# A two-layer decoder trunk on one core: masks written beside the rows and two tiles ahead, turnings of small tiles joined, key moves merged, the weight bound's passes regrouped

## Chip, core and metric

The kernel runs on one core of one Trainium2 chip. Its engines are named as in the profile: PE (TensorE matmul) and PEld (its weight load), DVE (VectorE), ACT (ScalarE), POOL (GpSimd) and SP (SyncE, which here only issues DMAs). The metric is the device time of one execution in microseconds (us), as the median over runs. A span is the time from the first to the last recorded instruction of a profiled execution.

## The reference

```python
D_MODEL, SEQ, DEPTH, N_MEM = 1024, 1024, 2, 256      # BATCH 1
FOX_HEADS, FOX_HEAD_DIM, MEM_HEADS, MEM_HEAD_DIM = 16, 64, 4, 128
...
def causal_multiscale_pool(u, pool_w, pool_scale): ...   # layer 0: trailing means of windows 2, 4, 8, 16
def shared_kv(x, w_kv_shared, b_forget): ...             # keys, values, cumulated log of the forget gates
def forgetting_attention(u, k, v, cum):
    # per head and block of 128 queries
    logits = q @ k.T * scale + (cum[t] - cum[s])
    logits = where(s <= t, logits, -inf)
    return softmax(logits) @ v
def memory_attention(q_mem, mem, w_mem_kv): ...          # 4 heads, softmax over 256 memory tokens
```

Each layer computes x = LayerNorm(alpha * x + W_out [main * silu(g_main); mem * silu(g_mem)]). In layer 0 main is the pooling branch, in layer 1 it is the forgetting attention (FoX) with 16 heads. Both layers have the memory attention.

## The kernel before

All products are made from operands split into a high part and a low part (and, in layer 0, a high part in another type), so that each product is a sum of two or three matmuls. A weight piece of 128x512 numbers is loaded into a buffer `raw` (four of them) or `B`, multiplied by a power of two in layer 1, and split. The power of two comes from a bound on the weights' absolute sums. This bound is worked out at run time: `look_ahead` (L231) loads a weight piece into one of eight slots in `lines[0]` by a DMA on POOL's queue (L240), seven pieces ahead, and has ACT sum the absolute values of the oldest (L244). There are 84 such pieces, 16 for the memory heads' weights and 68 for the others. `look_ahead` is called every 12 products in layer 0's output projection (L567) and at every eighth matmul of a slab (L327). After the last piece `send_bound(1)` (L267) sends the largest sum through DRAM to all partitions, and `scales_of_weights(1)` (L275) makes the scales from it in a chain of 12 small DVE instructions.

A slab (`slab`, L327) is 48 matmuls: one feature block of 128 columns of a weight matrix against all 1024 tokens. Keys (`k_units`), queries (`q_units`), values (`v_units`) and gates (`gate_units`) are slabs. Each is a generator that yields after each matmul, so slabs can be pumped in between other work.

Layer 0 has the pooling groups, the memory attention and the output projection `OutProj` (L512), whose `rest` ends with `norm` (L614). Layer 1 begins with the memory attention (`mem_attention`, L435): four query slabs in which the accumulators are evacuated by L431, L432 and L433, then for each of eight token tiles `probs` (L465 matmuls), a transposition, `values`, and four gate slabs as filling. Its outputs are multiplied by the gates on DVE (L509) and written to `y1d`. `scales_of_weights(1)` stands after it (L755). Then `start_units` runs: the first half of a key slab, `v_first` (the values of the first two pairs of heads and the forget logits, with weights in tiles MK; L804 is its matmul), the forget gates (L813 on), and the rest of the first pairs' keys and queries.

FoX (`fox`, L1043 on) runs over 16 heads, two to a pair, and over eight query tiles of 128 tokens in each, the largest (tile 7, 1024 keys) first. A step is one tile:

- `forget_rows` (L923) loads the next head's row of cumulated gates, in all partitions, into R (512 KB, L925, two buffers); this is called at the third tile of the head.
- `probs` (L928): POOL masks the diagonal block of R in place (L940), PE makes the logits in banks "L" (L295), one or two parts of up to 512 keys; DVE adds R and takes the least (L948) into a tile MK; ACT takes the exponential (L956) into a PSUM tile "T". The mask is held behind the mask of the tile before by `issue_after`.
- `halves`: ACT (L977) and DVE (L978) split the probabilities into a tile P, with the inverse of the sum (L966 or L968, then L969).
- `turn`: SP issues a DMA transposition of P into a tile T (L991). Tiles 2 and 0 are put behind tiles 3 and 1 in the same T.
- `values` (L1000): the products with V for four tiles at once; c=1 is tiles 4 to 7 (52 matmuls), c=0 is tiles 0 to 3. They come `LAG` = 5 steps behind, so that c=1 runs early in the next head's steps.
- `pair_out` (L1027): POOL multiplies the pair's outputs with the gates, SP writes them to `y1d` (L1029).

Between these, slabs of the coming pair are pumped in on PE. Their weights are split on POOL: L175 multiplies, L186 and L177 make the high and low halves. When a key slab is done, its halves have to lie in a second arrangement as well, high halves and low halves in other partitions: `move` (L858) does that with DMAs of 64 partitions on SP's queue. The keys' and queries' tiles are 16 lines of `lines[0]`, given out in turn by `qk`.

PE's order is written out by hand. The other engines' orders come from a scheduler, which also decides where DMAs stand in SP's and POOL's queues, except where an instruction is kept in program order or issued after another.

Of the kernel before, what the change touches and what calls it, by code (L numbers as in the profile page):

```python
# [12 lines left out]
F16 = mybir.dt.float16  # L13
# [65 lines left out]
def trunk_kernel(ctx, tc, x, xT, memT, win, wk, wv0, wv, wmk, wmv, wout, poolw, pscale, lng, lnb, bforget, out):  # L79
# [150 lines left out]

    def look_ahead():  # L231

        if lines:
            while len(landed) < 7:
                k, src = next(seen_of, (None, None))
                if k is None:
                    break
                r = lines[0][:, k % 8, :].bitcast(F32)
                r = r.rearrange("p (a b) -> p a b", a=4) if len(src.shape) == 3 else r[:, : src.shape[1]]
                nc.gpsimd.dma_start(r, src)  # L240
                landed.append((k, r))
            if landed:
                k, r = landed.pop(0)
                tc.keep_in_program_order(nc.scalar.activation(r, r, AF.Abs, accum_out=sums[:, k : k + 1]))  # L244
                if k == len(memory) + len(others) - 1:
                    send_bound(1)
# [50 lines left out]
    def slab(pieces_dram, X, evac, banks=("pj", 2)):  # L297
# [20 lines left out]
        for n, pc, part in order:  # L318
# [4 lines left out]
            for i in part:  # L323
                a, b = three(ws[pc], X)[i]
                for k in range(4):
                    seen[n] += 1
                    nc.tensor.matmul(  # L327
                        accs[n], a[:, k, :], b[:, pc * 4 + k, n * NH : (n + 1) * NH],
                        start=seen[n] == 1, stop=seen[n] == 3 * KT,
                    )  # L330
                    if sum(seen.values()) % 8 == 5:
                        look_ahead()
                    if seen[n] == 3 * KT:
                        evac(slice(n * NH, (n + 1) * NH), accs[n])
                    yield NH
# [99 lines left out]
    def mem_attention(l, X, kv, qtile, ytile, yd):  # L435
# [60 lines left out]
        with tc.manual_schedule(engines={PE}):  # L496
            for t in range(ST + 2):
                todo = [MVALUES if k in (5, 9) else 0 for k in range(t, ST + 2)]
                part = max(0, (fill.left + sum(todo)) / len(todo) - todo[0])
                if t < ST:  # L500
                    probs(t)
                fill.pump(part * 0.4)
                for h in range(MH):
# [8 lines left out]
    class OutProj:  # L512
# [39 lines left out]
        def products(self, accs, c, ys, apart=False):  # L552
# [9 lines left out]
            for a, nh, part in order:  # L562
                for i in part:
                    for k in range(4):
# [5 lines left out]
                        self.done += 1  # L570
                        if not self.l and self.done % 12 == 0:
                            look_ahead()
                        yield NH
# [160 lines left out]
    with tc.tile_pool(name="in1", bufs=1) as in1:  # L734
# [11 lines left out]

        line_at = [0]

        def qk():
            line_at[0] += 1  # L750
            return lines[0][:, line_at[0] % 16, :]

        kv = mem_kv(1)
        mem_attention(1, X, kv, xy, lambda: vt([P, S], F32), y1d[2])
        scales_of_weights(1)  # L755
        group[0] = 1
# [107 lines left out]
        def k_units(p):  # L864

            a, b, c, d = (qk() for _ in range(4))

            def evac(cols, acc):
                halves_out(a, b, cols, acc, QKSCALE)
                if cols.stop == S:  # L870
                    move(
                        (d, high64, a, high64), (c, low64, b, low64), (c, high64, a, low64), (d, low64, b, high64),
                        (a, high64, b, low64), (b, low64, d, high64),
                    )

            yield from slab(wk[p], X, evac)
            pairs[p] = [[(a, c), (b, d)]]

        def q_units(p):

            a, b, c = (qk() for _ in range(3))

# [37 lines left out]

        masked = []

# [5 lines left out]
        def probs(hd, i, R, sums, inverse, behind):  # L928
# [5 lines left out]
            q, kx, ky = pairs[hd // 2][hd % 2]  # L934
            L = (i + 1) * P
            qs = slice(i * P, L)
            p = MK([P, S], F32)
            with tc.issue_after(masked[-1]) if masked else nullcontext():
                masked.append(
                    nc.gpsimd.affine_select(R[:, qs], R[:, qs], [[-1, P]], ALU.is_ge, -NEG, base=0, channel_multiplier=1).ins  # L940
                )
            m = tiny(2)
            top = -NEG
            parts = [(0, L)] if L <= NH else [(0, 384), (384, L)] if L == 640 else [(0, NH), (NH, L)]
            for n, (lo, up) in enumerate(parts):
                lg = ps([P, NH], "L", 3)[:, : up - lo]
                mm3(lg, ((q[:, qs], kx[:, lo:up]), (q[:, qs], ky[:, lo:up])))
                nc.vector.tensor_tensor_reduce(p[:, lo:up], lg, R[:, lo:up], unq, top, ALU.add, ALU.min, m[:, n : n + 1])  # L948
                top = m[:, n : n + 1]
# [12 lines left out]
        def inverse_of(hd, i, n, sums):  # L962
# [7 lines left out]
            return r  # L970

        def halves(hd, i, es, r):

            L = (i + 1) * P
            pair = sb([P, 2 * S], "P", 4, F16)
            for lo, up, e in es:
# [6 lines left out]
        def turn(hd, i, two):  # L983

            n = 2 * i + 2
            if i in (2, 0):
                to = pt[hd, i + 1][:, n + 2 :, :]
            else:
                to = T([P, 2 * ST, P], F16)
            pt[hd, i] = to  # L990
            nc.sync.dma_start_transpose(to[:, :n, :], two[:, : n * P])  # L991
# [51 lines left out]
        def fox(following, out_proj):  # L1043
# [6 lines left out]

            ahead_R = forget_rows(0)
            for hd in range(HEADS + 1):
                pr, b = divmod(hd, 2)
# [15 lines left out]
                for i in range(ST if hd < HEADS else LAG):  # L1069
# [17 lines left out]
                    if i == 2 and hd < HEADS - 1:  # L1087
                        ahead_R = forget_rows(hd + 1)
                    if pr == 7:
                        step = b * ST + i  # L1090
# [100 lines left out]
```

## Time and profile before

| | us |
|---|---|
| median of 3 runs | 1229.65 |
| lowest and highest run | 1229.44, 1231.36 |
| the profiled execution's own time | 1231.59 |
| its span | 1229.9 |
| mean granted clock of PE, share of full speed | 0.988 |
| PE busy | 1181.9 |
| DVE busy | 777.1 |
| ACT busy | 700.8 |
| POOL busy | 266.6 |

The table is read as follows. The time of the profiled execution is 1.7 us over its span, since the work around the first and last instruction is not in the trace. Busy times of different engines overlap. An engine's busy time says how much it did and not whether another waited for it; for that one reads a wait and what released it. The order of the views in the next part follows this: whole span, stretches, waits, timeline.

In the profile "L" and a number is a line of the kernel before. "P<-T,s,P 128x512" names the output tile, the inputs and the shape of the output. "x4" counts instructions that follow each other. Brackets hold the engine's idle time ahead of the first of them, and what ended it.

### The profile page before, as it was taken

The page shows a single profiled execution, that of the slowest core. Times are in us where ns is not written, and L with a number is a line of the kernel's source. Part 1 is how long each engine was busy: PE and PEld are TensorE (multiplying, and loading weights), DVE is VectorE, ACT ScalarE, POOL GpSimd, SP SyncE. Part 2 cuts the span into 40 slices and gives each one's busy share as a digit, 9 for nine tenths or more (in the row PEclk, how much of TensorE's full clock was granted, in tenths as well). Part 3 has the DMA queues.
Part 4 walks back from the last instruction along what each step waited for, and adds up shares of the span by engine and source line. Part 5 has one row for each costly group of instructions (what it writes and reads, how often), then busy time and mean ns, then how long its engine had stood idle before and what let it go on. Part 6 is the DMA issues. An engine that isn't in the chain of part 4 may idle for free. (4 is left out here: it accounts for less than half of the span.)

```text
span 1229.9 us, 20105 instructions
## 1 busy us (share of the span) xinstructions
PE 1181.9 (96%) x7018; PEld 683.3 (56%) x7018; DVE 777.1 (63%) x1811; ACT 700.8 (57%) x1556; POOL 266.6 (22%) x437
## 2 busy tenths in 40 slices
PE   8999999999999998999799998998999999999997
PEld 4566676555555666556474455544455555455553
DVE  7534776375645467367743877667777878773754
ACT  6555774374574455787331776556666767685220
POOL 4000000000122110210243444443333422640000
PEclk9999999999999999999899999999999999999999
DMA  6233553243695655574825878976975887796340
GB/s 226 85 114 96 119 134 137 86 120 95 208 347 181 195 195 162 187 226 102 262 90 147 168 151 212 181 176 153 214 176 119 176 169 165 213 227 196 136 151 37
DMA packets 276773, 200.90 MB, mean 163 GB/s; under 512 B 213920, under 2 KB 227360, under 8 KB 276672
## 3 DMA queue, kind: packets, MB, share of 16 engines
q1 hardware_dynamic: 270080, 178.45, 54.7%
q0 software_dynamic: 6592, 21.17, 5.1%
q8 instruction: 55, 0.90, 0.3%
q14 instruction: 46, 0.38, 0.1%
HBM read 116.14 MB, written 22.61 MB: 113 GB/s over the span
## 5 line engine op out<-in xcount | busy, mean ns | idle before, releaser
L327 PE MATMUL pj<-A,w 128*128 128x512 f16 (+2 forms) x2928 | 673.3, 384 | 10.7 <-ACT w L171 5.3
L327 PEld LDWEIGHTS <-w 128*128 128x128 f16 (+1 forms) x2592 | 249.5, 98 | 290.1 <-issue 11.8
L956 ACT ACTIVATE T<-MK,s 128x512 f32<-128x512 f32 x192 | 111.4, 580 | 75.6 <-DVE s L948 59.3
L977 ACT ACTIVATE P<-T,s 128x512 f16<-128x512 f32 x192 | 102.3, 576 | 63.6 <-issue 33.1
L978 DVE SCALAR_TENSOR_TENSOR P<-T,s,P 128x512 f16<-128x512 f32 x192 | 111.7, 613 | 33.9 <-ACT P L977 32.8
L567 PEld LDWEIGHTS <-T 128*128 128x128 bf16 x736 | 71.0, 98 | 86.9 <-issue 6.0
L240 POOL DMA_DIRECT2D A<-in_win_dram x48 | 26.4, 551 | 372.2 <-PE pj L327 304.5
L192 DVE TENSOR_TENSOR w<-raw,w 128x512 bf16<-128x512 f32 x84 | 60.4, 720 | 61.6 <-PE pj L327 35.7
L295 PE MATMUL L<-A 128*128 128x512 f16 (+3 forms) x384 | 85.3, 326 | 8.3 <-DVE s L948 6.3
L948 DVE CUSTOM_DVE_ANT_0 MK<-L,R,scales 128x512 f32<-128x512 f32 (+3 forms) x128 | 80.3, 628 | 18.2 <-DMA R<-cumd 8.4
L327 PEld LDWEIGHTS pj<-A,w 128*128 128x128 f32 x368 | 69.3, 190 | 20.2 <-ACT A L191 3.6
L940 POOL TENSOR_SCALAR_AFFINE_SELECT R<-R 128x128 f32<-128x128 f32 x128 | 37.1, 296 | 170.9 <-DVE s L948 117.1
L1000 PE MATMUL O<-T,V 128*64 128x128 f16 (+1 forms) x1152 | 60.5, 227 | 10.0 <-DMA T<-P 9.8
L1000 PEld LDWEIGHTS <-V 128*64 128x64 f16 (+1 forms) x1152 | 53.5, 108 | 26.7 <-issue 12.4
L295 PEld LDWEIGHTS <-A 128*128 128x128 f16 x384 | 37.1, 98 | 52.3 <-issue 10.4
L191 ACT CAST w<-raw 128x512 fp32r<-128x512 f32 x84 | 52.0, 619 | 21.0 <-PE pj L327 12.0
L192 DVE TENSOR_TENSOR T<-T,T 128x1024 bf16<-128x1024 f32 x23 | 28.0, 1218 | 56.4 <-ACT T L191 41.8
L177 POOL TENSOR_TENSOR w<-B,w 128x512 f16<-128x512 f32 x54 | 62.4, 1156 | 3.5
L193 ACT CAST w<-raw 128x512 bf16<-128x512 f32 x84 | 52.0, 619 | 13.0 <-PE pj L327 12.4
L175 POOL TENSOR_SCALAR B<-B,scales 128x512 f32<-128x512 f32 x54 | 41.1, 774 | 83.6 <-DVE scales L285 29.8
L191 ACT CAST T<-T 128x1024 fp32r<-128x1024 f32 x23 | 24.1, 1046 | 57.4 <-DMA T<-y1d 36.2
L567 PE MATMUL pj<-B,T 128*128 128x512 bf16 (+1 forms) x192 | 54.3, 393 | 0.0
(263 smaller groups left out, 1796.0 us busy)
## 6 DMA issues: line engine op xcount, KB each, us to landing
raw<-in_win_dram SPq DMA_DIRECT2D x66, 256.0 KB, 2.8
A<-in_win_dram POOLq DMA_DIRECT2D x48, 256.0 KB, 5.2
raw<-in_wout_dram SPq DMA_DIRECT2D x40, 256.0 KB, 2.7
A<-A SPq DMA_DIRECT2D x72, 128.0 KB, 2.7
R<-cumd SPq DMA_DIRECT2D x16, 512.0 KB, 4.6
B<-in_win_dram SPq DMA_DIRECT2D x15, 512.0 KB, 4.8
y0d<-Y SPq DMA_DIRECT2D x12, 512.0 KB, 2.9
T<-y0d SPq DMA_DIRECT2D x12, 512.0 KB, 4.8
```

The lines of the kernel that those rows point to most:

```text
L177: nc.gpsimd.tensor_tensor(to.lo, src, to.hi, ALU.subtract)
L191: pin(nc.scalar.copy(to.hi, src))
L192: pin(nc.vector.tensor_tensor(to.lo, src, to.hi.bitcast(F32), ALU.subtract))
L193: (top or nc.scalar.copy)(to.top, src)
L295: nc.tensor.matmul(acc, a, b, start=i == 0, stop=i == len(terms) - 1)
L327: nc.tensor.matmul(accs[n], a[:, k, :], b[:, pc * 4 + k, n * NH : (n + 1) * NH], start=seen[n] == 1, stop=seen[n] == 3 * KT,)
L567: nc.tensor.matmul(accs[a][nh], y, w, start=kt == 8 and i == 0, stop=kt == 7 and i == 2,)
L948: nc.vector.tensor_tensor_reduce(p[:, lo:up], lg, R[:, lo:up], unq, top, ALU.add, ALU.min, m[:, n : n + 1])
L956: nc.scalar.activation(e, p[:, lo:up], AF.Exp, bias=top, scale=-1.0, accum_out=sums[:, n, hd % 2, i : i + 1],)
L977: nc.scalar.activation(pair[:, lo:up], e, AF.Copy, scale=r)
L978: nc.vector.scalar_tensor_tensor(pair[:, L + lo : L + up], e, r, pair[:, lo:up], ALU.mult, ALU.subtract)
L1000: nc.tensor.matmul(acc[rows, (i % 4) * P : (i % 4) * P + P], v[:, b, 2 * j : 2 * j + (1 if e else 2), :].rearrange("p e d -> p (e d)"), pt ...
```

## The change

The change has five parts.

1. `look_ahead` takes an argument. In layer 0's output projection it is called from product 36 on instead of 12, still every 12 products, and until product 48 it only loads. In slabs it is called at every sixth matmul instead of every eighth.
2. `scales_of_weights(1)` is called inside the memory attention, after the probabilities of the eighth tile, and no longer behind it.
3. Keys and queries lie in fixed lines of `lines[0]`: `8 * (p % 2) + k`, with k = 0 to 3 for keys and 4 to 6 for queries. The keys' second arrangement is made by three DMAs of two lines each, in place of six DMAs of one line.
4. The mask no longer writes R. `mask` writes the whole last part of a tile's row (128 to 512 columns, the diagonal block being its last 128) into a `raw` tile C, which DVE reads for that part in R's place. The masks are issued two tiles ahead, and no longer held behind the one before.
5. Tiles 3 and 2 share one tile P, and so do tiles 1 and 0; `turn` issues one transposition for both, when the second is done.

```diff
--- before.py
+++ after.py
@@ -228,7 +228,7 @@
     sums = const.tile([P, len(memory) + len(others)], F32, name="sums")
     seen_of, landed, lines = iter(enumerate(memory + others)), [], []
 
-    def look_ahead():
+    def look_ahead(see=True):
 
         if lines:
             while len(landed) < 7:
@@ -239,7 +239,7 @@
                 r = r.rearrange("p (a b) -> p a b", a=4) if len(src.shape) == 3 else r[:, : src.shape[1]]
                 nc.gpsimd.dma_start(r, src)
                 landed.append((k, r))
-            if landed:
+            if landed and see:
                 k, r = landed.pop(0)
                 tc.keep_in_program_order(nc.scalar.activation(r, r, AF.Abs, accum_out=sums[:, k : k + 1]))
                 if k == len(memory) + len(others) - 1:
@@ -328,7 +328,7 @@
                         accs[n], a[:, k, :], b[:, pc * 4 + k, n * NH : (n + 1) * NH],
                         start=seen[n] == 1, stop=seen[n] == 3 * KT,
                     )
-                    if sum(seen.values()) % 8 == 5:
+                    if sum(seen.values()) % 6 == 5:
                         look_ahead()
                     if seen[n] == 3 * KT:
                         evac(slice(n * NH, (n + 1) * NH), accs[n])
@@ -499,6 +499,8 @@
                 part = max(0, (fill.left + sum(todo)) / len(todo) - todo[0])
                 if t < ST:
                     probs(t)
+                if l and t == ST - 1:
+                    scales_of_weights(1)
                 fill.pump(part * 0.4)
                 for h in range(MH):
                     if todo[0]:
@@ -568,8 +570,8 @@
                             accs[a][nh], y, w, start=kt == 8 and i == 0, stop=kt == 7 and i == 2,
                         )
                         self.done += 1
-                        if not self.l and self.done % 12 == 0:
-                            look_ahead()
+                        if not self.l and self.done >= 36 and self.done % 12 == 0:
+                            look_ahead(self.done >= 48)
                         yield NH
 
         def early(self, y, ys):
@@ -744,15 +746,8 @@
         def vt(shape, dt=F32R):
             return sb(shape, "V", 4, dt, in1)
 
-        line_at = [0]
-
-        def qk():
-            line_at[0] += 1
-            return lines[0][:, line_at[0] % 16, :]
-
         kv = mem_kv(1)
         mem_attention(1, X, kv, xy, lambda: vt([P, S], F32), y1d[2])
-        scales_of_weights(1)
         group[0] = 1
         cumd = dram.tile([HEADS, S], F32, name="cumd")
         fg = G((P, 8, ST * HEADS))
@@ -863,22 +858,19 @@
 
         def k_units(p):
 
-            a, b, c, d = (qk() for _ in range(4))
+            own, odd = (lines[0][:, k : k + 2, :] for k in (8 * (p % 2), 8 * (p % 2) + 2))
 
             def evac(cols, acc):
-                halves_out(a, b, cols, acc, QKSCALE)
+                halves_out(own[:, 0], own[:, 1], cols, acc, QKSCALE)
                 if cols.stop == S:
-                    move(
-                        (d, high64, a, high64), (c, low64, b, low64), (c, high64, a, low64), (d, low64, b, high64),
-                        (a, high64, b, low64), (b, low64, d, high64),
-                    )
+                    move((odd, high64, own, high64), (odd, low64, own, high64), (own, high64, own, low64))
 
             yield from slab(wk[p], X, evac)
-            pairs[p] = [[(a, c), (b, d)]]
+            pairs[p] = [[(own[:, 0], own[:, 1]), (odd[:, 0], odd[:, 1])]]
 
         def q_units(p):
 
-            a, b, c = (qk() for _ in range(3))
+            a, b, c = (lines[0][:, 8 * (p % 2) + k, :] for k in (4, 5, 6))
 
             def evac(cols, acc):
                 halves_out(a, b, cols, acc, -QKSCALE)
@@ -918,7 +910,21 @@
             yield from own
             yield from islice(following, 48)
 
-        masked = []
+        def parts_at(i):
+
+            L = (i + 1) * P
+            return [(0, L)] if L <= NH else [(0, 384), (384, L)] if L == 640 else [(0, NH), (NH, L)]
+
+        diagonal = {}
+
+        def mask(hd, i, R):
+
+            lo, up = parts_at(i)[-1]
+            C, w = raw([P, NH]), up - lo
+            nc.gpsimd.affine_select(
+                C[:, :w], R[:, lo:up], [[-1, w]], ALU.is_ge, -NEG, base=w - P, channel_multiplier=1,
+            )
+            diagonal[hd, i] = C
 
         def forget_rows(hd):
             R = sb([P, S], "R", 2, F32, in1)
@@ -932,20 +938,16 @@
 
 
             q, kx, ky = pairs[hd // 2][hd % 2]
-            L = (i + 1) * P
-            qs = slice(i * P, L)
+            qs = slice(i * P, (i + 1) * P)
             p = MK([P, S], F32)
-            with tc.issue_after(masked[-1]) if masked else nullcontext():
-                masked.append(
-                    nc.gpsimd.affine_select(R[:, qs], R[:, qs], [[-1, P]], ALU.is_ge, -NEG, base=0, channel_multiplier=1).ins
-                )
+            C, parts = diagonal.pop((hd, i)), parts_at(i)
             m = tiny(2)
             top = -NEG
-            parts = [(0, L)] if L <= NH else [(0, 384), (384, L)] if L == 640 else [(0, NH), (NH, L)]
             for n, (lo, up) in enumerate(parts):
                 lg = ps([P, NH], "L", 3)[:, : up - lo]
                 mm3(lg, ((q[:, qs], kx[:, lo:up]), (q[:, qs], ky[:, lo:up])))
-                nc.vector.tensor_tensor_reduce(p[:, lo:up], lg, R[:, lo:up], unq, top, ALU.add, ALU.min, m[:, n : n + 1])
+                rows = C[:, : up - lo] if n == len(parts) - 1 else R[:, lo:up]
+                nc.vector.tensor_tensor_reduce(p[:, lo:up], lg, rows, unq, top, ALU.add, ALU.min, m[:, n : n + 1])
                 top = m[:, n : n + 1]
                 if n == 0:
                     inverse()
@@ -969,10 +971,17 @@
             nc.vector.reciprocal(r, r)
             return r
 
+        joined = []
+
         def halves(hd, i, es, r):
 
             L = (i + 1) * P
-            pair = sb([P, 2 * S], "P", 4, F16)
+            if i in (2, 0):
+                pair = joined.pop()[:, 2 * L + 2 * P :]
+            else:
+                pair = sb([P, 2 * S], "P", 4, F16)
+                if i in (3, 1):
+                    joined.append(pair)
             for lo, up, e in es:
                 nc.scalar.activation(pair[:, lo:up], e, AF.Copy, scale=r)
                 nc.vector.scalar_tensor_tensor(pair[:, L + lo : L + up], e, r, pair[:, lo:up], ALU.mult, ALU.subtract)
@@ -983,11 +992,14 @@
         def turn(hd, i, two):
 
             n = 2 * i + 2
+            if i in (3, 1):
+                joined.append(two)
+                return
+            to = T([P, 2 * ST, P], F16)
+            pt[hd, i] = to
             if i in (2, 0):
-                to = pt[hd, i + 1][:, n + 2 :, :]
-            else:
-                to = T([P, 2 * ST, P], F16)
-            pt[hd, i] = to
+                pt[hd, i + 1], pt[hd, i] = to, to[:, n + 2 :, :]
+                n, two = 2 * n + 2, joined.pop()
             nc.sync.dma_start_transpose(to[:, :n, :], two[:, : n * P])
 
         def values(hd, c, o):
@@ -1049,6 +1061,8 @@
                 fill.add(gate_units(win[1, 12 + pr], gs[pr], X), SLAB, True)
 
             ahead_R = forget_rows(0)
+            for i in range(2):
+                mask(0, ST - 1 - i, ahead_R)
             for hd in range(HEADS + 1):
                 pr, b = divmod(hd, 2)
                 if hd == HEADS:
@@ -1086,6 +1100,10 @@
 
                     if i == 2 and hd < HEADS - 1:
                         ahead_R = forget_rows(hd + 1)
+                    if i < ST - 2 and hd < HEADS:
+                        mask(hd, tile_of - 2, R)
+                    elif hd < HEADS - 1:
+                        mask(hd + 1, 2 * ST - 3 - i, ahead_R)
                     if pr == 7:
                         step = b * ST + i
                         if step in (0, 1, 5, 11):
```

## The prediction

> **What bounds the kernel now.** I read the page's first part, then a table by stretches, then PE's waits, then the timeline where a wait is long.
>
> ```profile
> span 1229.9 us, 20105 instructions
> PE 1181.9 (96%) x7018; PEld 683.3 (56%) x7018; DVE 777.1 (63%) x1811; ACT 700.8 (57%) x1556; POOL 266.6 (22%) x437
> ```
>
> PE is busy for all but 48.0 us. The change takes no matmul away, so it can win only those holes and the time lost to a low granted clock. The stretches show where they lie (start and end, length, busy time of PE, PEld, DVE, ACT and POOL, PE's granted clock, DMA share, GB/s): the step into the FoX stage, the whole FoX stage, a part of it with DMA at its densest, and the output projection.
>
> ```profile
> 604.00:617.00 13.00, 7.76 (x29) 3.29 (x30) 11.83 (x25) 4.99 (x10) 8.38 (x10) 0.74 0.73 257
> 668.00:1096.00 428.00, 406.70 (x2829) 215.59 (x2828) 320.29 (x931) 284.24 (x681) 171.78 (x296) 0.99 0.79 176
> 840.00:890.00 50.00, 44.70 (x324) 24.59 (x322) 37.90 (x112) 33.07 (x81) 18.73 (x33) 0.97 0.90 183
> 1096.00:1230.00 134.00, 124.72 (x583) 70.91 (x581) 71.16 (x123) 38.59 (x57) 5.36 (x6) 0.98 0.43 143
> ```
>
> PE idles 5.2 us in the first and 21.3 in the second (428.00 less 406.70), and no other engine is near its limit there. The 9.3 of the last stretch the change does not touch. What ends PE's waits between 600 and 1110 (total, times, longest):
>
> ```profile
> PE O L1000 <- DMA T<-P: 9.8, 4, 3.1
> PE L L295 <- DVE s L948: 6.3, 9, 1.3
> PE pj L327 <- ACT w L171: 5.3, 1, 5.3
> PE L L295 <- DMA A<-A: 1.6, 1, 1.6
> ```
>
> Three things can be won: one wait for the split key weights, the waits for turned probabilities, and small ones for logits' evacuation and moved keys.
>
> **Part A, the scales of layer 1's weights, moved ahead into the memory attention.** The timeline at its end (start, length, engine, line, tiles; in brackets the idle time before and its releaser):
>
> ```profile
> 605.12 2.35 DVE L509 TENSOR_TENSOR V<-V,G 128x1024 f32<-128x1024 f32 x2
> 608.47 1.33 ACT L171 ACTIVATE w<-raw,scales 128x512 f16<-128x512 f32 x2 [10.21 <-DVE scales L282]
> 609.24 7.41 PE L327 MATMUL pj<-A,w 128*128 128x512 f16 x24 [5.31 <-ACT w L171]
> 608.62 17.50 POOL L175 TENSOR_SCALAR B<-B,scales 128x512 f32<-128x512 f32 x20 [29.76 <-DVE scales L285]
> 610.95 3.46 DVE L172 SCALAR_TENSOR_TENSOR MK<-raw,scales,MK 128x272 f16<-128x272 f32 x4
> 617.34 0.50 DVE L172 SCALAR_TENSOR_TENSOR MK<-raw,scales,MK 128x272 f16<-128x272 f32 x1 [0.39 <-ACT MK L171]
> 616.49 1.72 PE L804 MATMUL pj<-MK,A 128*128 128x272 f16 x13
> 500.25 10.52 PE L327 MATMUL pj<-A,w 128*128 128x512 f16 x48
> ```
>
> The scales now queue on DVE behind the last L509; ACT's split waits 10.21 for them and PE 5.31. With the scales in the eighth tile's step, the split is done before PE gets there: 5.31 go. The 24 matmuls behind the hole took 7.41; 48 undisturbed ones take 10.52, so 24 take 5.26: 2.15 more, for the clock. At most 7.46 is won.
>
> What is late next: PE reaches the slab at 603.93, leaves it 5.26 later and wants the low halves of `v_first` (L172 into MK) 8 matmuls after that, at 0.13 each: 610.2. In the built program's order DVE makes four of them behind L509, which ends at 607.47. At 0.50 each they end at 609.5, in time. But POOL's L175, 0.875 us each, then runs beside them, since it has its scales early too. Should the two L509 and the four L172 each wait for one L175, that is 5.3 more. So 0 to 5.3 late; I take the middle, 2.7: A = -4.8 (-7.5 to -2.2).
>
> The trace shows L172 at 0.87 each in the row of four and 0.50 alone, both beside POOL. The Trainium skill ("SBUF — State Buffer", section "Who interferes with whom") has DVE instructions with two SBUF inputs shut out by a GpSimd instruction reading SBUF, for the whole of it. A DVE instruction that comes at a random moment would then wait half of 0.875, 0.44 more, which agrees with 0.87. By that alone the four would end at 611.2 and A would be about -6.5. The same section lets DVE instructions with one SBUF input pass; L948 and L978 read PSUM and one tile of SBUF, so POOL's wider masks would not slow them.
>
> **Part B, the bound's passes (ACT Abs, L244).** In layer 0's output projection the first passes begin at product 48 and not 12, the loads at 36. In the built program the first load waits for the same matmul count as before, since its buffer must come free, so PE's hole there stays; it is for the norm's vector, whose load DVE's L260 awaits just ahead of the L192 that PE needs:
>
> ```profile
> 339.56 1.12 PE L567 MATMUL L<-B,T 128*128 128x512 bf16 x4 [2.57 <-DVE T L192]
> 337.15 1.22 DVE L260 TENSOR_REDUCE scales<-P 128x1 f32<-128x1024 f32 x1 [1.15 <-DMA P<-in_lnb_dram]
> 497.08 0.62 ACT L244 ACTIVATE A<-A 128x512 f32<-128x512 f32 x1
> 497.72 0.69 ACT L431 ACTIVATE B<-pj,scales 128x512 fp32r<-128x512 f32 x1
> 499.53 0.67 ACT L433 ACTIVATE B<-pj,scales 128x512 bf16<-128x512 f32 x1
> ```
>
> I cost the projection at nothing: ACT is far from full, and if that cover were gone it would be one 0.62 per pass ahead of a cast, with some four places. Every sixth matmul in place of every eighth puts eight passes, not six, into each query slab of the memory attention. The order shows one more Abs ahead of L431, which began at 497.72 as the Abs before it ended; L433 ended at 500.20 and PE's next slab began at 500.25. So the accumulator comes free 0.62 later, at three of the slab ends: up to 1.9, nothing if ACT finds the room elsewhere. I take three quarters, B = +1.4 (0 to 1.9), as the slab followed L433 with no slack. The passes end sooner in the gates' slabs.
>
> **Part C, FoX: masks, turnings, key moves.** One place in a head with a long wait, and the totals:
>
> ```profile
> 724.49 1.36 POOL L175 TENSOR_SCALAR B<-B,scales 128x512 f32<-128x512 f32 x2 [5.58 <-DMA B<-in_wv_dram]
> 725.82 1.41 POOL L1027 TENSOR_TENSOR G<-G,G 128x256 f32<-128x256 f32 x2
> 727.18 0.29 POOL L940 TENSOR_SCALAR_AFFINE_SELECT R<-R 128x128 f32<-128x128 f32 x1
> 727.51 0.54 DVE L948 CUSTOM_DVE_ANT_0 MK<-L,R,s 128x256 f32<-128x256 f32 x1 [2.71 <-POOL R L940]
> 838.50 0.54 DVE L948 CUSTOM_DVE_ANT_0 MK<-L,R,s 128x256 f32<-128x256 f32 x1 [0.89 <-POOL R L940]
> POOL R L940 <- DVE s L948: 117.1, 52, 5.8
> DVE MK L948 <- POOL R L940: 14.8, 9, 3.5
> ```
>
> POOL stands 5.58 us at a weight's DMA, does gates, and only then the mask that DVE wants; POOL's masks in turn wait 117.1 us for DVE's earlier evacuations, because they write R in place. Where it shows on PE:
>
> ```profile
> 694.71 2.47 PE L1000 MATMUL O<-T,V 128*64 128x128 f16 x52 [1.34 <-DMA T<-P]
> 743.06 4.06 PE L1000 MATMUL O<-T,V 128*64 128x128 f16 x52 [3.14 <-DMA T<-P]
> 854.15 2.48 PE L1000 MATMUL O<-T,V 128*64 128x128 f16 x52 [2.67 <-DMA T<-P]
> 880.02 3.88 PE L1000 MATMUL O<-T,V 128*64 128x128 f16 x52 [2.62 <-DMA T<-P]
> ```
>
> The 52 products wait for tile 4's turning. The mask waits at 727.51 and 838.50 lie about 15.6 us ahead of the second and third, two tiles before tile 4 on DVE. With masks two tiles ahead and no write into R, POOL is that much earlier. I count 2.71 and 0.89, and 1.59 of slow clock at 743.06 (4.06 less 2.47). The clock at 880.02 and the holes at 694.71 and 880.02 I leave: no mask wait stands two tiles ahead of them. The key moves go from six DMAs, three deep, to three, two deep, so the 1.6 for A<-A goes; and one of nine waits on L948 behind the mask at 838.50, 0.7. C = -7.5. At best all four waits, both slow clocks (1.59 and 1.41) and the keys go: -14.4.
>
> What is added:
>
> ```profile
> L940 POOL TENSOR_SCALAR_AFFINE_SELECT R<-R 128x128 f32<-128x128 f32 x128 | 37.1, 296 | 170.9 <-DVE s L948 117.1 <-DVE s L969 40.0 <-DVE s L968 12.6
> L186 POOL TENSOR_SCALAR w<-B 128x512 f16<-128x512 f32 x54 | 33.8, 626 | 42.9 <-PE pj L327 42.9
> L177 POOL TENSOR_TENSOR w<-B,w 128x512 f16<-128x512 f32 x54 | 62.4, 1156 | 3.5
> ```
>
> Masks copy 2688 columns a head, not 1024. No row has a mask of 512 columns; L186 and L177 bound it at 0.63 and 1.16, so 2688 columns cost 3.3 to 6.1 us a head, less the 2.3 of now: +16 to +60 over 16 heads, nearer the first, as it has one input. POOL at 171.78 of 428 has room; if not, the price is again a mask wait. Joining tiles 3 with 2 and 1 with 0 makes six turnings of eight a head. Tile 3's now waits for tile 2, but its products already wait for tile 0's, so it costs nothing; if that fails, it is one landing:
>
> ```profile
> R<-cumd SPq DMA_DIRECT2D x16, 512.0 KB, 4.6
> cumd<-G SPq DMA_DIRECT2D x8, 8.0 KB, 2.4
> T<-P SPq DMA_TRANSPOSE x144, 3.7
> ```
>
> Masks take the raw buffers; the output projection's early weight loads move to the last head for it, still ahead of their use.
>
> **Sum.** -4.8 + 1.4 - 7.5 = -10.9. The profiled execution took 1231.59 (span 1229.9 and 1.7 around it), 1.94 over the median of 1229.65. So 1220.7 by the profiled one and 1218.7 against the median.
>
> **Rivals.** R1, the masks come no earlier: POOL takes its work in order, and a mask behind an L175 that waits 5.58 for its DMA is late two tiles ahead too. For it: that wait; against: most masks wait for DVE, and two tiles are 6.7 us (428.00 over 128 tiles, twice). Only the keys' 1.6 is left of C: 1229.65 - 4.8 + 1.4 - 1.6 = 1224.7.
>
> R2, `v_first` takes the whole of A: DVE is held by POOL as bounded above, and by late raw loads. Speaking for it is 0.87 against 0.50; against, a loss of 7.5 is over the bound. A = 0: 1223.6.
>
> R3, slower: in the built program's SP order, the next head's R (512 KB) goes out right behind the joined turning, so ahead of tile 5's and tile 4's in nearly every head; before, it went out behind tile 4's. It costs what a 512 KB load lands later than an 8 KB one, 4.6 less 2.4 = 2.2, and decides where R's packets are still queued when tile 4's turning is issued and PE has no slack. That is four heads that wait already and three that I count within 0.7 us of it: 7 x 2.2 = 15.4. For it: DMA at 0.90 between 840 and 890; against: sixteen engines share the packets, and other heads have slack of some us. C = -7.5 + 15.4 = +7.9: 1229.65 - 4.8 + 1.4 + 7.9 = 1234.2.
>
> **How the numbers follow.** Forecast 0.59, R1 0.13, R2 0.07, R3 0.21. The forecast's own range is 1210 to 1225; with the rivals, and with half of R3's neighbourhood left out, 1209 to 1232. A measurement tells 0.2% (2.5 us) from no change. R1 and R2 are faster by more than that; R3 is 4.5 us slower, and a part-way R3 gives the share of no change: 0.73, 0.08, 0.19.
>
> **What would show it.** A: PE's 5.3 wait on L171 is gone, and a wait on L172 into MK of at most 5.3 stands at 610. B: PE's query slabs 0.6 further apart. C: the mask waits of 14.8 near zero, POOL's 117.1 gone, the waits on T<-P half. R3 would show waits on T<-P in more than four heads, tile 4's turning landing later than 3.7 behind its issue. Slow clock stretches in FoX that the sum does not name would prove the whole sum wrong.

## The result and the profile after

| | before | changed |
|---|---|---|
| median of 4 runs, us | 1230.51 | 1218.99 |
| lowest and highest | 1229.44, 1233.81 | 1217.23, 1220.1 |
| the profiled execution's own time | 1231.59 | 1219.56 |
| its span | 1229.9 | 1217.9 |

The ratio of the times is 0.9901, 95% interval 0.9877 to 0.9924. The forecast was 1218.7, so the total was met. It was counted from 1229.65; from the 1230.51 above, the drop is 11.5 against the 10.9 that were forecast. The terms under the total were not all met, and the rest of this document is about them.

The page's first part of the changed kernel, then its stretches (same columns as before the change: start and end, length, busy time of PE, PEld, DVE, ACT, POOL, PE's granted clock, DMA share, GB/s). The second stretch is the FoX stage alone, from its first logits to its last product with V:

```profile
span 1217.9 us, 20007 instructions
PE 1177.5 (97%) x7018; PEld 679.8 (56%) x7018; DVE 775.0 (64%) x1811; ACT 700.0 (57%) x1556; POOL 291.4 (24%) x437
...
604.00:617.00 13.00, 11.76 (x117) 8.10 (x117) 12.58 (x16) 3.37 (x7) 13.00 (x13) 1.00 0.92 326
668.00:1091.31 423.31, 410.96 (x2876) 217.82 (x2877) 323.81 (x936) 289.10 (x689) 196.91 (x298) 1.00 0.83 185
840.00:890.00 50.00, 47.36 (x343) 25.23 (x342) 39.60 (x119) 34.85 (x86) 21.79 (x34) 1.00 0.93 199
```

The same stage of the kernel before:

```profile
670.00:1103.33 433.33, 413.63 (x2876) 219.24 (x2877) 324.81 (x936) 288.63 (x687) 174.63 (x299) 0.99 0.79 178
```

PE makes the same 2876 products in both. FoX is 10.02 shorter: PE's idle time fell from 19.70 to 12.35, and its busy time by 2.67, which is time at the low clock: the rows of 4.06 and 3.88 us for 52 matmuls before, one such row after. What PE still waits for after 660, and what DVE and POOL wait for there, in the changed kernel:

```profile
PE O L1012 <- DMA T<-P: 7.8, 6, 3.3
PE L L295 <- DVE s L950: 3.2, 6, 0.9
PE pj L569 <- DVE G L342: 1.0, 1, 1.0
PE L L295 <- DMA A<-A: 0.3, 1, 0.3
...
POOL raw L924 <- DVE s L950: 85.1, 42, 4.5
...
DVE MK L950 <- DMA R<-cumd: 7.2, 1, 7.2
```

DVE no longer waits for a mask anywhere (14.8 before). But the waits for turned probabilities fell only from 9.8 to 7.8, and now are six.

To compare stages, I read seven moments from PE's timeline in each kernel: the start of the first query slab of layer 1, the end of the products with the memory's weights (L363) that follow the fourth, the last product of the memory attention, the first product of `v_first`, the first transposition after it, FoX's first logits, and FoX's last product. Lengths in us:

| | query slabs | memory attention | wait and key slab | v_first | to FoX | FoX |
|---|---|---|---|---|---|---|
| before | 52.51 | 64.28 | 12.56 | 22.29 | 31.22 | 433.33 |
| changed | 54.21 | 66.63 | 5.02 | 24.63 | 29.91 | 423.31 |
| B alone | 54.21 | 67.51 | 11.97 | 23.44 | 31.36 | 431.79 |
| changed without B | 52.51 | 64.73 | 5.02 | 26.41 | 29.46 | 420.96 |
| A alone | 52.51 | 64.78 | 5.02 | 26.55 | 31.21 | 430.83 |
| C alone | 52.52 | 64.36 | 13.37 | 22.68 | 29.65 | 422.74 |
| masks alone | 52.51 | 64.23 | 13.46 | 22.70 | 31.04 | 430.07 |
| joined turnings alone | 52.51 | 64.23 | 12.64 | 22.24 | 30.39 | 425.99 |
| key moves alone | 52.51 | 64.00 | 13.43 | 22.70 | 29.46 | 431.87 |
| masks alone, R held | 52.51 | 64.22 | 12.54 | 22.30 | 30.45 | 420.99 |
| changed, R held | 54.21 | 67.31 | 5.02 | 25.15 | 29.76 | 418.04 |
| changed without B, R held | 52.51 | 64.57 | 5.02 | 27.02 | 29.53 | 418.45 |
| the same, gate products deferred | 52.51 | 65.20 | 5.02 | 27.09 | 29.46 | 418.12 |
| the same, half the weights in B | 52.51 | 63.27 | 5.02 | 26.47 | 30.46 | 420.29 |

The rows behind the changed kernel are explained with the experiments. Each row is one profiled execution; those of masks alone and of B alone took 5.5 and 3.8 more than the median of their kernel, that of A alone 2.8 less. Where two kernels run the same FoX program, the stage differs by up to 2.5 (433.33, 431.79, 430.83; 423.31, 420.96, 422.74), so smaller differences of that column say nothing. The other columns repeat to some tenths where the program is the same, save that a stretch of low clock can add about one.

Against the kernel before, the changed one gives: A (key slab and `v_first`) -7.54 + 2.34 = -5.20. B (query slabs and memory attention) 1.70 + 2.35 = +4.05. C (to FoX and FoX) -1.31 - 10.02 = -11.33. With +0.46 ahead of the query slabs that is -12.02, the difference of the spans.

### The profile page after: what moved, and what is told of

Read it like the earlier page. It is cut to its first block, busy times and chain, and to the rows that moved or that the text cites. A ratio compares the mean times of both kernels' runs of the same rounds, so it can differ in the third digit from the quotient of the medians.

```text
span 1217.9 us, 20007 instructions
## 1 busy us (share of the span) xinstructions
PE 1177.5 (97%) x7018; PEld 679.8 (56%) x7018; DVE 775.0 (64%) x1811; ACT 700.0 (57%) x1556; POOL 291.4 (24%) x437
## 5 line engine op out<-in xcount | busy, mean ns | idle before, releaser
L924 POOL TENSOR_SCALAR_AFFINE_SELECT raw<-R 128x256 f32<-128x256 f32 (+3 forms) x128 | 59.7, 469 | 133.7 <-DVE s L950 85.1
L175 POOL TENSOR_SCALAR B<-B,scales 128x512 f32<-128x512 f32 x54 | 43.1, 810 | 82.8 <-DVE scales L285 30.6
L950 DVE CUSTOM_DVE_ANT_0 MK<-L,R,scales 128x512 f32<-128x512 f32 x64 | 45.5, 711 | 16.2 <-PE L L295 8.9
```

Of the source, the lines that this page charges most:

```text
L924: nc.gpsimd.affine_select(C[:, :w], R[:, lo:up], [[-1, w]], ALU.is_ge, -NEG, base=w - P, channel_multiplier=1,)
```

## The experiments

Ratios are to the kernel before, run beside them on the same chip, with 95% intervals.

**B alone** (the diff's hunks of `look_ahead`, the slab and the output projection, on the kernel before).

```diff
-                    if sum(seen.values()) % 8 == 5:
+                    if sum(seen.values()) % 6 == 5:
...
-                        if not self.l and self.done % 12 == 0:
-                            look_ahead()
+                        if not self.l and self.done >= 36 and self.done % 12 == 0:
+                            look_ahead(self.done >= 48)
```

> The kernel before with part B alone (the bound's passes begin later, every sixth matmul). If the passes cost only PE's three holes of 0.33 and the 0.3 behind them at layer 1's query slabs, the time rises by about 1.7 us, to 1232, and nothing follows after them. If the passes also put ACT's and DVE's chain of the memory attention behind PE, as the waits of 1.3 on L494 and 2.1 on the last turning in the changed kernel suggest, it rises by 3 to 4.5, to 1234 or so, and these two waits stand in this kernel too.

Median 1234.18, ratio 1.0032 (1.0009 to 1.0054): slower, by 3.9 from the ratio. PE's timeline of this kernel, at the second query slab and in the memory attention:

```profile
503.15 10.52 PE L327 MATMUL pj<-A,w 128*128 128x512 f16 x48 [0.32 <-ACT B L433]
...
577.93 0.96 PE L465 MATMUL L<-MK,B 128*128 128x256 f32 x6 [1.12 <-ACT P L471]
584.39 1.50 PE L295 MATMUL T<-T,MK 128*128 128x128 f16 x24 [1.49 <-DVE V L494]
606.68 0.49 PE L295 MATMUL T<-T,MK 128*128 128x128 f16 x6 [1.42 <-DMA T<-P]
```

The first hole is the one that was predicted; with it the query slabs stand 0.57 further apart. The three below it were not predicted: the kernel before has only one wait there, 0.88 for a turning. They come from the chain of softmax steps on ACT and DVE, and the trace shows where that chain falls behind. Counted from the end of the query slabs' stage, ACT's exponentials of the fourth token tile begin as early as before (23.47 against 23.48), those of the fifth 3.85 later (33.18 against 29.33). Between them ACT waits for a tile P, which is still being read by the second token tile's transposition:

```profile
559.63 1.60 SPq L482 DMA_TRANSPOSE T<-P  x1
560.73 0.54 POOL L271 DMA_DIRECT2D line<-s  x1 [19.88 <-DVE s L468]
572.49 1.71 ACT L477 ACTIVATE P<-P,s 128x256 f16<-128x256 f32 x4 [3.42 <-DMA T<-P]
```

This transposition landed 12.76 behind its issue, against 4.56 in the kernel before. The passes end sooner, and so does what follows them: the bound goes out to DRAM (L271) 1.1 behind the second tile's transposition, and not, as before, 1.3 behind the fourth's. In the three kernels profiled with B the second transposition took 11.2 to 12.8, in the eleven without B 4.4 to 4.7. So B brings these waits by itself. Whether the bound's write or another transfer of these microseconds holds the transposition up was not tried apart.

**The changed kernel without B.**

```diff
-                    if sum(seen.values()) % 6 == 5:
+                    if sum(seen.values()) % 8 == 5:
```

and the old start in the output projection.

> The changed kernel with part B undone (every eighth matmul and from product 12 on, as before). If B costs 1.7 us: 1217.3. If it also costs the waits in the memory attention: 1214.5 to 1216. If the scales' earlier place needs the bound earlier, so that A depends on B: a wait on the scales comes back and the time is 1219 or more.

Median 1215.79, ratio 0.9885 (0.9865 to 0.9905), against 0.9901 for the changed kernel: the medians differ by 3.2, the intervals overlap. The stages are clearer: query slabs and memory attention together are 3.60 shorter, and 1.78 of it are lost again in `v_first`. The scales are there in time, so A does not need B.

**A alone.**

```diff
+                if l and t == ST - 1:
+                    scales_of_weights(1)
...
-        scales_of_weights(1)
         group[0] = 1
```

> The kernel before with the scales' place alone changed. If the wait of 5.3 and the slow clock's 2.1 go, less some 1.8 of waits at the first values: -5.6, about 1225. If the two waits in the memory attention come from the scales' chain in DVE's row: -3, about 1227.5. If the first values take it all: 1230.5.

Median 1228.54 of 12 runs from 1223.58 to 1233.31, ratio 0.9986 (0.9968 to 1.0003): not told from no change by its times. By its stages A wins 7.54 on the key slab and loses 4.26 on `v_first` and 0.50 in the memory attention: -2.78.

**R held behind tile 4's turning**, on the changed kernel.

```diff
-        joined = []
+        joined, turned = [], [None]
...
-            nc.sync.dma_start_transpose(to[:, :n, :], two[:, : n * P])
+            issued = nc.sync.dma_start_transpose(to[:, :n, :], two[:, : n * P])
+            if i == 4:
+                turned[0] = issued.ins
...
-                        ahead_R = forget_rows(hd + 1)
+                        with tc.issue_after(turned[0]) if turned[0] else nullcontext():
+                            ahead_R = forget_rows(hd + 1)
```

> The changed kernel with each head's row R (512 KB) held behind the turning of tile 4 on SP's queue, nothing else. If R's packets are what makes tile 4's turning land late (3.0 to 6.7 us behind its issue in the changed kernel, 2.9 to 5.6 before): landings of about 3.5 in most heads, the 7.8 us of PE's waits on it fall to 3 or less, 1214 to 1216. If other transfers (weights, gates' outputs) or the chain ahead of the issue set it: 1218 to 1220, with the landings as they were.

Median 1215.99, but with one run at 1225.73, so that the ratio is 0.9900 (0.9871 to 0.9928), the same as the changed kernel's: by the times the hold is not shown to be worth anything here. In the profiled executions FoX took 418.04 against 423.31, and PE's waits on turnings 4.7 against 7.8, where 3 or less was expected. SP's queue in the first head, first the changed kernel's and then this one's (start, length, engine, line, operation):

```profile
685.20 0.74 SPq L931 DMA_DIRECT2D R<-cumd  x1
686.05 1.52 SPq L1003 DMA_TRANSPOSE T<-P  x1
687.66 0.54 SPq L304 DMA_DIRECT2D B<-in_win_dram  x1
688.86 5.49 SPq L1003 DMA_TRANSPOSE T<-P  x2
```

```profile
689.98 2.12 SPq L1003 DMA_TRANSPOSE T<-P  x1
692.16 0.58 SPq L931 DMA_DIRECT2D R<-cumd  x1
692.92 2.24 SPq L1003 DMA_TRANSPOSE T<-P  x1
```

The turning issued at 688.86 is tile 4's. In the changed kernel it landed 5.97 later, with R's 512 KB ahead of it; here, issued at 689.98, 3.81 later. Not all landings shorten: the mean over the 16 heads goes from 4.39 to 3.97 (3.55 before the change).

**Masks alone, joined turnings alone, key moves alone**, each as its hunks of the diff on the kernel before.

> The kernel before with the masks alone out of place and two tiles ahead. In its built order R stands ahead of tile 5's and tile 4's turning, as in the changed kernel. If the masks carry FoX's gain and R's new place costs what holding it back saved (5.7 in the FoX stage): FoX shorter by 3 to 6 of the 10, time 1225 to 1228, tile 4's turnings landing at 4.4 on average against 3.55. If the masks carry all of it: 1221. If they only paid together with the joined turnings: 1230 or more.

> The kernel before with the turnings of tiles 3 and 2 and of 1 and 0 joined, nothing else; R stays behind tile 4's turning. If two turnings less a head free SP's queue and the DMA engines for tile 4's: FoX shorter by 2 to 4, 1227 to 1229. If they have no part: 1231 within noise. If joining makes a turning late: slower, with waits on c=0's turning, which before had 4 us and more of slack.

> The kernel before with the keys' and queries' fixed lines and three moves in place of six. The wait of 1.6 at FoX's start falls to 0.3; inside FoX three DMAs less a pair give 0 to 2. 1228 to 1229.5. If moves and not masks made the gain between heads 4 and 8 (7.5 of FoX's 10): 1222.

Masks: 1227.91, ratio 0.9967 (0.9947 to 0.9988). Joined: 1226.06, 0.9960 (0.9944 to 0.9975). Keys: 1231.27, 1.0006 (0.9992 to 1.0021). PE's waits in FoX, masks alone and then joined alone:

```profile
PE O L1010 <- DMA T<-P: 12.3, 8, 4.0
PE L L295 <- DVE s L958: 4.7, 5, 1.8
```

```profile
PE L L295 <- DVE s L948: 7.0, 7, 1.7
PE O L1010 <- DMA T<-P: 6.4, 5, 3.0
```

With the masks alone DVE never waits for one, and yet PE waits no less for turnings than before (12.3 against 9.8; 4.0 of the 12.3 is one wait in the last head, where no R is loaded any more). Tile 4's turning landed 4.12 behind its issue on average, against 3.55 before. Joining, which leaves the masks as they were, lowers that wait, and DVE's waits on masks with it:

```profile
DVE MK L948 <- POOL R L940: 9.3, 8, 2.3
```

That is 14.8 before. The key moves give 1.76 ahead of FoX, nothing that can be seen in it, and nothing that can be seen in the time, which was expected at 1228 to 1229.5.

**Masks alone with R held**, the hold above on the kernel with the masks alone.

> The kernel before with the masks alone changed, and each R held behind tile 4's turning. With the masks alone the FoX stage took 430.1 and PE waited 12.3 for turnings. If R's early place takes back what the masks give: FoX 425 to 427, the waits on turnings at 6 or less, time 1222 to 1226. If masks are worth little by themselves: 1228 as without the hold.

Median 1221.12, ratio 0.9923 (0.9901 to 0.9946); without the hold 0.9967 (0.9947 to 0.9988). These just do not overlap: R's place took 0.44% from the masks, some 5.4 us. Tile 4's turning landed at 3.61 on average, FoX is 12.3 shorter than before, and PE's waits on turnings are

```profile
PE O L1012 <- DMA T<-P: 4.4, 4, 1.8
```

**C alone** (masks, joined turnings and key moves on the kernel before).

> The changed kernel's masks, joined turnings and key moves on the kernel before, without A and B. By the stages of the profiles A wins 2.8 to 3 alone and B loses 4, so that A and B together give about -1 and C gives about -11: 1219 to 1221, no slower than the changed kernel by more than 1.5. If C needs A or B: 1223 or more.

Median 1223.08, ratio 0.9930 (0.9911 to 0.9949), above what was expected. Its FoX and the step to it are those of the changed kernel within 0.6; 2.5 of the profile's time lies ahead of layer 1's query slabs, where the program is the one before. Whether A and B together are worth the 4.1 between the two medians or the 1.2 to 2.4 of the stages stays open. PE's waits in FoX with C alone:

```profile
PE O L1011 <- DMA T<-P: 10.4, 9, 1.9
PE L L295 <- DVE s L949: 2.9, 5, 0.9
```

**Both repairs together, and two tries at `v_first`.** First B undone and R held; then the memory attention's last gate products on DVE issued behind `v_first`'s weights:

```diff
-        for h in range(MH):
-            nc.vector.tensor_tensor(ys[h], ys[h], gs[h], ALU.mult)
-            nc.sync.dma_start(yd[:, h, :], ys[h])
+        def gated():
+            for h in range(MH):
+                nc.vector.tensor_tensor(ys[h], ys[h], gs[h], ALU.mult)
+                nc.sync.dma_start(yd[:, h, :], ys[h])
+
+        if l:
+            return gated
+        gated()
...
                 scaled_hi_lo(ws[kt // 4][:, kt % 4, :], r, sws[1])
+            gated()
```

and last the second half of the weights in tiles of B as well (`for of in (MK, xy)`).

> The changed kernel with part B undone and each R held behind tile 4's turning. If the two costs lie in different stages and add (3.2 to 4 and 3 to 5.7): 1210 to 1213. If the noise of the single runs hid that one of them was nothing: 1215 to 1216.

> The changed kernel with B undone, R held behind tile 4's turning, and the memory attention's last gate products (the TENSOR_TENSOR of V and G on DVE) issued behind v_first's weights, so that the four late low halves stand ahead of the last two. If these products are what makes the first values wait (4.2 us in the stage): v_first 24 to 25 against 27, 1210 to 1212 against 1213. If POOL's splits or the memory tile's release do: as without, 1213.

> As the kernel with the deferred gate products, and the second half of v_first's weights in tiles of B, which are free some 10 us before the memory attention's values let go of MK. If the tile's release sets the wait: v_first at 22.3 to 23.5 as in the kernel before, 1208.5 to 1211. If raw loads or POOL set it: 1211 to 1213.

Medians 1213.18, 1212.33 and 1213.96; ratios 0.9869 (0.9844 to 0.9893), 0.9851 (0.9829 to 0.9872) and 0.9868 (0.9846 to 0.9890). The second is faster than the changed kernel beyond both intervals; the three do not differ among themselves. The first came out at the upper edge of what was expected; both tries missed, with `v_first` at 27.09 and 26.47 after 27.02. The deferred kernel's DVE and PE show why:

```profile
607.73 3.48 DVE L172 SCALAR_TENSOR_TENSOR MK<-raw,scales,MK 128x272 f16<-128x272 f32 x4
611.13 2.76 DVE L512 TENSOR_TENSOR V<-V,G 128x1024 f32<-128x1024 f32 x2
613.82 0.77 DVE L172 SCALAR_TENSOR_TENSOR w<-raw,scales,w 128x512 f16<-128x512 f32 x1
614.51 0.68 DVE L863 SCALAR_TENSOR_TENSOR A<-pj,A 128x512 f16<-128x512 f32 x1
...
615.24 9.94 PE L805 MATMUL pj<-MK,A 128*128 128x272 f16 x70 [2.78 <-DVE A L863]
```

The low halves come in time, but the gate products now stand ahead of L863, which empties the key slab's accumulator, and PE waits 2.78 for that; with half the weights in B it waits 2.40 for the same. DVE and POOL are nearly full here (12.58 and 13.00 of 13.00 in the changed kernel's stretch): these two orders moved the wait and did not remove it.

## Why the prediction was right, and where it was not

**A, -4.8.** Right in mechanism; the size hangs on B. PE's wait on L171 is gone with its slow clock. What was to be late next is late: `v_first` is 2.34 longer in the changed kernel, and 4.12 and 4.26 without B, inside the 0 to 5.3. So A is -5.20 in the changed kernel, where B brings PE here some 4 us later and DVE has that much more time, and -2.8 to -3.4 without B; that the forecast's middle was hit is in part luck. The prediction found no other engine near its limit; its own row has DVE busy for 11.83 of 13.00 in this stretch. The rows of the changed kernel:

```profile
608.29 5.34 PE L327 MATMUL pj<-A,w 128*128 128x512 f16 x24
613.47 0.97 PE L799 MATMUL pj<-MK,A 128*128 128x272 f16 x7
615.12 1.06 PE L799 MATMUL pj<-MK,A 128*128 128x272 f16 x7 [0.67 <-ACT MK L171]
616.75 0.28 PE L799 MATMUL pj<-MK,A 128*128 128x272 f16 x1 [0.57 <-DVE MK L172]
617.60 20.66 PE L799 MATMUL pj<-MK,A 128*128 128x272 f16 x177 [0.57 <-DVE MK L172]
```

**B, +1.4 (0 to 1.9).** Mis-sized. The query slabs lost 1.70, as worked out. The step that failed is "The passes end sooner in the gates' slabs", taken as free: with them the bound's write moves beside the second tile's transposition, which takes 6.6 more to land in the changed kernel (11.19 against 4.56), and the memory attention lost 2.35 more, for 4.05.

**C, -7.5.** Right in sign, short by 3.8, and wrong in what carries it. Three steps failed.

First, joining "costs nothing" and, by silence, wins nothing. Alone it takes 0.40% off the time, about as much as the masks alone (0.33%); in the FoX stage it is 7.34 and the masks alone 3.26, and C alone has 10.59. So over the whole the two gains add, within the noise of one execution each (by the times 0.33% and 0.40% against 0.70%). They do not in the stretch from the first product with V of head 3 to that of head 7, which took 112.25 before and 104.78 in the changed kernel: there either one by itself wins as much (103.08 joined, 104.43 masks). A reading that fits this stretch is a loop: SP's queue late, weights land late, POOL's L175 late, mask late, DVE late, turning late, SP later. The runs show that either cut suffices there and that joining lowers the waits on masks; the loop's single links were not cut one by one, and why joining pays is so far argued.

Second, the waits on turnings as the place where the gain shows. The two that were priced did fall, by 2.04 and 1.34 where 2.71 and 0.89 were counted, and the slow clock at 743.06 is gone (the mask waits before them are those of tile 5, one tile ahead of tile 4 and not two, as the prediction read). But head 0's rose, two small ones are new, and all together fell by only 2.0; with C alone they are 10.4, no less than before. What fell instead: the waits on logits' evacuation by 3.1 (6.3 to 3.2; 0.7 was counted), and 1.5 on L767 and 0.7 on L862, not counted, went away. Slow clock gave 2.67, not 1.59.

Third, R. The rival R3 was priced at 2.2 a head on seven heads, and given 0.21 as an alternative. It is no alternative: it happened along with the gain. Both signs named for it came, waits on turnings in more than four heads (six) and tile 4's turning landing later than 3.7 (4.39 on average). R does stand ahead of tile 4's turning, since masks out of place let go of its buffer sooner (it is the row of the head after next, not of the next as the prediction said), and it took about 5.4 from the masks alone. The changed kernel's waits at tile 4's turning:

```profile
694.88 3.83 PE L1012 MATMUL O<-T,V 128*64 128x128 f16 x52 [3.31 <-DMA T<-P]
742.56 2.47 PE L1012 MATMUL O<-T,V 128*64 128x128 f16 x52 [1.10 <-DMA T<-P]
846.15 2.48 PE L1012 MATMUL O<-T,V 128*64 128x128 f16 x52 [1.33 <-DMA T<-P]
870.66 2.48 PE L1012 MATMUL O<-T,V 128*64 128x128 f16 x52 [1.31 <-DMA T<-P]
```

These are heads 0, 2, 6 and 7. In the last three the waits are a third to a half of what they were (3.14, 2.67, 2.62), but head 0's went from 1.34 to 3.31, with a stretch of low clock behind it (3.83 for the 52 products). The prediction took such a stretch, named by no term, as a sign against its whole sum.

**R1** did not come true: no wait of DVE on a mask is left. **R2** came true in part: `v_first` took 2.34 of A's 7.54 in the changed kernel and more than half without B, and A alone is not told from no change by its times.

**POOL's masks** cost 59.7 instead of 37.1, +22.6, near the lower end of 16 to 60 that was chosen:

```profile
L924 POOL TENSOR_SCALAR_AFFINE_SELECT raw<-R 128x512 f32<-128x512 f32 x32 | 19.6, 612 | 26.7 <-DVE s L950 23.8 <-DVE s L971 1.5 <-DMA R<-cumd 1.4
```

The Trainium skill ("SBUF — State Buffer", section "Who interferes with whom") lets DVE instructions with one SBUF input pass beside GpSimd. Here L950 of 512 columns took 744 ns on average, and L948 before 745 ns: no run shows POOL's wider masks slowing it, as that rule has it.

So the total was met by luck, as two errors cancelled: B cost 2.6 more than said, C won 3.8 more.

## What to carry to other kernels

When a change frees a buffer earlier, ask which transfer then starts earlier, and which landing that PE awaits it gets ahead of; holding one 512 KB load behind the turning that PE waits for was worth 0.44% with the masks alone, more than the masks had brought without it (0.33%), though on the whole changed kernel the times do not show it. Do not put a part of a change at nothing because it costs nothing: run each alone and all together, since gains can add over the whole and overlap in one stretch. When passes end sooner, what waits for their end moves too: ask which transfer then goes out, and beside which one that an engine awaits.

## What was not expected of the hardware

In the changed kernel the turning of tile 4 landed 3.0 us behind its issue in three of the 16 heads and 5.6 to 6.7 in heads 0, 3, 4 and 7. The 512 KB load does not decide this alone: it was still under way in heads 0 and 3, but also in heads 1, 11 and 13, where the turning took 3.0, 3.8 and 3.4, and in heads 4 and 7 it had landed before the turning was issued. The write of the bound, 0.5 KB, took 6.9 to 11.4 us to land in the fourteen kernels. The mask of 512 columns on POOL took 612 ns against 292 for 128 columns: four times the columns at twice the time.
